# A two-layer diffusion backbone: the conditioning and first block of layer 0 traced in another order, with five pieces of the conditioning multiplied whole

## The chip, the cores and the metric

The kernel runs on one core of a Trainium2 chip, in one launch. The metric is device time in microseconds (us), as a median over runs. TensorE (PE) multiplies matrices, VectorE (DVE), ScalarE (ACT) and GpSimd (POOL) work element by element, SyncE (SP) issues nearly all transfers; each takes its instructions in order.

## The reference

The model has width 1024 and two layers over 256 context tokens and 2048 latent tokens. What matters here is how a layer starts: a conditioning vector goes through SiLU and a 1024 x 3072 matrix (`ada_w`), which gives shift, scale and gate; the input is normed, scaled and shifted to h; h goes into the layer's projections. All is float32.

```python
def ada_mod(cvec, w, b):
    m = jax.nn.silu(cvec) @ w + b
    shift, scale, gate = jnp.split(m, 3, axis=-1)
    return shift[:, None], scale[:, None], gate[:, None]

def modulate(x, mod, g):
    shift, scale, _ = mod
    return rmsnorm(x, g) * (1 + scale) + shift

def reference(...):
    for l in range(DEPTH):                       # 2 layers
        mp = ada_mod(c_ctx[None], ada_w[l], ada_b[l])
        ms = ada_mod(c, ada_w[l], ada_b[l])
        hp = modulate(xp, mp, norm_pre[l])       # 256 context tokens
        hs = modulate(xs, ms, norm_pre[l])       # 2048 latent tokens
        # l = 0: mla_pool_mixer (latent attention and pooling), l = 1: swa_mixer (banded attention)
        ...
        xp = xp + mp[2] * rmsnorm(op, norm_post[l])
        xs = xs + ms[2] * rmsnorm(os_, norm_post[l])
```

## The kernel before

Everything is kept transposed, features on the 128 partitions, so x is 8 chunks of 128 features. Tokens come in nine blocks of 256; block 0 is the context. Layer 0 makes two passes over the blocks: the first projects h to the low-rank queries, keys and values and to the pooling branch (chunks 0 to 4, the small matrix `wkr`, chunks 9 to 12 of `w0`), the second, with h made again, to the gates. Then comes attention, the output projection, and layer 1 in the same manner.

A float32 product is made from three float32r products: each operand is split into a high part, a rounded copy made on ScalarE, and a low part, the difference, made on VectorE or GpSimd (`split`, L55 to L57); `mm3` (L110) multiplies high by high, high by low and low by high. float32r matmuls are quick; a matmul on plain float32 operands needs no split.

The conditioning of layer 0 (L357 to L363) needs 16 pieces of `ada_w`, each 256 x 512 and 512 KB: four column groups j (2 and 3 hold the scale, 0 and 1 the shift, half of the features each), four quarters q of the 1024 rows. Each piece is loaded into one of 12 staging buffers (`wload`, L118), split, and multiplied with the SiLU of the two conditioning vectors by four matmuls (`ada_piece`, L137). After the fourth quarter of a group ScalarE copies the row out (`adarow`, L150), TensorE transposes it (L153), and VectorE adds the bias and, for the scale groups, forms (1 + scale) times the norm's weight (`amod`, L160). I number the pieces 0 to 15 in the order in which they are traced: groups 2, 0, 3, 1.

Block 0's h is made between them. `h_stats` (L168) loads x, squares it on ScalarE in two halves, adds the squares up on GpSimd, sums over the partitions with one fp32 matmul against ones (L186), forms r = 1/sqrt(mean square) in `rstd_of` (L90 to L100), stores r for the second pass (L188) and multiplies x by r (L190): on GpSimd for block 0, on VectorE for all later blocks. `h_mod` (L193) makes the high part as x m + s on ScalarE (L199), x m + s again on VectorE (L200), and the low part as their difference (L201). The buffer of x is single, so block 1's x is loaded when block 0's h is made. The buffer `sq` of the squares is single as well.

The text of the kernel doesn't fix the order of the instructions. A scheduler, which simulates a timeline of its own, sets for each engine and for SP's queue in what order they stand; instructions given to `keep_in_program_order` are not moved ahead. Semaphores carry the dependences. Before, the five loads of `w0` for chunks 0 to 4 and their splits (`w_in_load`, L366 to L370) are traced after all pieces, with low parts in turn on VectorE and GpSimd, and `h_mod` of block 0 after them.

## Time and profile before

| | |
|---|---|
| median of three runs | 3144.53 us (3138.21 to 3149.47) |
| the profiled execution | 3137.79 us, span 3135.7 us |
| mean granted TensorE clock | 0.984 of 2.4 GHz |
| busy share of the span | TensorE 96%, VectorE 70%, ScalarE 57%, GpSimd 50% |
| transfers | 375 MB, 120 GB/s on average, nearly all on SP's queue |

The span is the time from the first to the last instruction of the profiled execution; its own device time is 2 us longer. A busy share is an average over stages; the windows show it stage by stage. The timeline lists instructions by start, with the idle time before them and what ended it. A matmul's place in the pipe is best read from the distance between starts. An fp32 matmul shows as two records (x2).

### The profile page before, as it was taken

How to read it: one execution, taken by the hardware profiler on the slowest of the kernel's cores; microseconds unless marked ns; L12 is line 12 of the kernel's file. 1: busy time of each engine (PE TensorE's matmuls, PEld its weight loads, DVE VectorE, ACT ScalarE, POOL GpSimd, SP SyncE). 2: the span in 40 equal slices, each digit the busy share in tenths (PEclk: the TensorE clock that was granted, in tenths of full speed). 3: DMA queues.
4: the chain of work that ended last, by engine and by line, in shares of the span. 5: the costliest groups of instructions: out<-in, count | busy, mean ns of one | idle time of the engine just before them, and what ended most of it. 6: DMA issues, size and time to landing. Idle time of an engine off the chain costs nothing.

```text
span 3135.7 us, 53071 instructions
## 1 busy us (share of the span) xinstructions
PE 3001.8 (96%) x19120; PEld 2580.0 (82%) x19120; DVE 2183.6 (70%) x3976; ACT 1772.6 (57%) x3571; POOL 1579.3 (50%) x1406
## 2 busy tenths in 40 slices
PE   6999999999999999999999999999997999999998
PEld 4999988897777777777779999999996677666998
DVE  6656656986888888888856646677324888867555
ACT  6444444435877777777774433333324777775433
POOL 3223232215777787777875435555002555545554
PEclk8999999999999999999999999999998999999999
DMA  6544468743202202222215564436437354541554
GB/s 236 155 138 138 150 188 256 234 145 93 60 19 56 61 16 58 58 47 58 59 42 161 161 200 143 137 127 203 143 94 149 82 105 105 117 84 48 158 173 126
DMA packets 379681, 375.08 MB, mean 120 GB/s; under 512 B 27905, under 2 KB 344953, under 8 KB 378265
## 3 DMA queue, kind: packets, MB, share of 16 engines
q1 hardware_dynamic: 379404, 371.68, 41.8%
q8 instruction: 150, 2.46, 0.3%
q14 instruction: 115, 0.93, 0.1%
q10 hardware_dynamic: 12, 0.00, 0.0%
HBM read 242.13 MB, written 129.24 MB: 118 GB/s over the span
## 4 chain that ended last, share of the span: by engine, by line
PE 61%; DVE 12%; DMA 12%; ACT 5%; POOL 5%; issue 4%; SPq 1%; DVEq 0%; ACTq 0%; POOLq 0%
PE S L114 5%; PE S L115 5%; PE S L113 5%; PE S L598 4%; PE B L643 4%; PE A L640 4%; PE S L599 4%; PE S L600 4%; PE M L552 4%; PE M L114 3%; PE M L115 3%; PE M L113 3%; PE S L1172 2%; PE S L1171 2%; DVE xb L200 1%
## 5 line engine op out<-in xcount | busy, mean ns | idle before, releaser
L630 POOL TENSOR_TENSOR acc<-acc,ph 128x512 f32<-128x512 f32 x352 | 457.5, 1300 | 58.3 <-ACT ph L602 39.3
L602 ACT ACTIVATE ph<-S 128x512 fp32r<-128x512 f32 (+1 forms) x592 | 350.4, 592 | 177.9 <-PE S L600 170.0
L553 DVE TENSOR_REDUCE pm<-M 128x1 f32<-128x512 f32 (+1 forms) x656 | 390.9, 624 | 80.4 <-PE M L552 77.8
L614 DVE TENSOR_TENSOR pl<-S,ph 128x512 fp32r<-128x512 f32 (+1 forms) x496 | 334.3, 676 | 70.8 <-ACT S L607 63.2
L113 PE MATMUL S<-hh,wh 128*128 128x256 f32 x1296 | 370.2, 286 | 4.4 <-ACT wh L56 2.8
L114 PE MATMUL S<-hl,wh 128*128 128x256 f32 x1296 | 368.8, 285 | 4.1 <-DVE hl L201 4.1
L115 PE MATMUL S<-hh,wl 128*128 128x256 f32 x1296 | 368.7, 285 | 0.0
L607 ACT ACTIVATE S<-S 128x512 f32<-128x512 f32 (+1 forms) x496 | 292.0, 589 | 0.0
L113 PEld LDWEIGHTS S<-hh,wh 128*128 128x128 f32 x1296 | 249.3, 193 | 8.7 <-ACT wh L56 3.3
L114 PEld LDWEIGHTS S<-hl,wh 128*128 128x128 f32 x1296 | 249.8, 193 | 6.4 <-DVE hl L201 4.8
L115 PEld LDWEIGHTS S<-hh,wl 128*128 128x128 f32 x1296 | 249.5, 193 | 1.6 <-issue 0.3
L598 PE MATMUL S<-QS,KHL 97*128 97x512 f32 (+1 forms) x592 | 235.5, 398 | 2.0 <-DVE pl L614 1.3
L599 PE MATMUL S<-QS,KHL 96*128 96x512 f32 (+1 forms) x592 | 233.9, 395 | 0.0
L643 PE MATMUL B<-pl,VV 128*65 128x512 f32 (+1 forms) x592 | 228.7, 395 | 3.8 <-ACT ob L658 2.3
L600 PE MATMUL S<-QS,KHL 96*128 96x512 f32 (+1 forms) x592 | 232.3, 392 | 0.0
L552 PE MATMUL M<-KHL,QS 96*128 96x512 f32 (+1 forms) x656 | 221.2, 378 | 1.3 <-DVE pm L553 1.0
L640 PE MATMUL A<-ph,VV 128*128 128x512 f32 (+1 forms) x592 | 212.2, 397 | 2.5 <-ACT ph L602 2.0
L1189 POOL TENSOR_TENSOR bpl<-bpf,bph 128x512 fp32r<-128x512 f32 x136 | 178.0, 1309 | 58.0 <-ACT bpf L1177 50.4
L113 PE MATMUL M<-hh,oh 128*128 128x256 f32 x696 | 196.4, 283 | 3.3 <-ACT oh L56 3.3
L114 PE MATMUL M<-hl,oh 128*128 128x256 f32 x696 | 195.0, 280 | 0.0
L115 PE MATMUL M<-hh,ol 128*128 128x256 f32 x696 | 194.8, 280 | 0.0
L1181 POOL TENSOR_SCALAR_AFFINE_SELECT bpf<-bpf 128x512 f32<-128x512 f32 x120 | 79.5, 663 | 199.8 <-ACT bpf L1177 176.3
(380 smaller groups left out, 9496.9 us busy)
## 6 DMA issues: line engine op xcount, KB each, us to landing
q_d<-ehl SPq DMA_DIRECT2D x126, 256.0 KB
stg<-in_ada_w SPq DMA_DIRECT2D x48, 512.0 KB
xb<-in_xT SPq DMA_DIRECT2D x18, 1024.0 KB
xb<-x_d SPq DMA_DIRECT2D x18, 1024.0 KB
stg<-in_w SPq DMA_DIRECT2D x35, 512.0 KB
hh<-q_d SPq DMA_DIRECT2D x24, 512.0 KB
kn_d<-ehl SPq DMA_DIRECT2D x40, 256.0 KB
v_d<-ve SPq DMA_DIRECT2D x20, 512.0 KB
```

Of the source, the lines that this page charges most:

```text
L113: pe.matmul(ps, lhsT=wh, rhs=xh, start=i == 0, stop=False)
L114: pe.matmul(ps, lhsT=wh, rhs=xl, start=False, stop=False)
L115: pe.matmul(ps, lhsT=wl, rhs=xh, start=False, stop=i == n - 1)
L552: pe.matmul(ps[:, :w], lhsT=QS[u % 4][0:96, 0, 128 * s:128 * s + 128], rhs=KH[h % 2][0:96, c0:c0 + w], start=True, stop=True)
L553: dve.tensor_reduce(out=pms[u][:, s, i:i + 1], in_=ps[:, :w], axis=AX.X, op=ALU.max)
L598: pe.matmul(S[:, :n], lhsT=KH[s][0:97, kc], rhs=qh, start=True, stop=False)
L599: pe.matmul(S[:, :n], lhsT=KH[s][0:96, kc], rhs=ql[0:96], start=False, stop=False)
L600: pe.matmul(S[:, :n], lhsT=KL[s][0:96, kc], rhs=qh[0:96], start=False, stop=True)
L602: act.activation(out=ph[:, :n], in_=S[:, :n], func=AF.Exp, scale=MLA_SCALE)
L630: pool.tensor_tensor(out=acc[:, :n], in0=acc[:, :n] if ph0 is None else f(ph0)[:, :n], in1=f(ph)[:, :n], op=ALU.add)
L640: pe.matmul(A[:, :n], lhsT=V[:, kts[i], 0:128], rhs=ph[:, :n], start=i == 0, stop=i == nk - 1)
L643: pe.matmul(B[0:65, :n], lhsT=V[:, kts[i], 64:129], rhs=pl[:, :n], start=i == 0, stop=i == nk - 1)
```

## The change

All loads and steps of layer 0's conditioning and of block 0's h, and the first five loads of `w0`, now stand in one function, `first_block`, in a written order, and a new context `in_order` ties every instruction in it to the one before it on the same engine. The instructions of SP count too.

- Loads: `cs` first, then three pieces, then `ident`, `adab`, `vecs`, the fourth piece, x of block 0 and the other pieces. The store of r is traced before the five loads of `w0`. Loads for what follows are not issued before the last of `first_block` (`issue_after`).
- Five pieces (3, 7, 11, 14, 15) are not split: two fp32 matmuls each on the loaded data.
- The squares of block 0: GpSimd adds two pairs of chunks, four fp32 matmuls against ones add the rest, instead of one.
- h, for all blocks of both layers: VectorE forms (x m) r by chunk in one step (`h_scale`), ScalarE adds s for the high part, VectorE forms (x + s) minus the high part (`h_parts`). GpSimd no longer scales block 0.
- The low parts of `w0`'s first five chunks are all on VectorE.
- The sink loads of layer 1 and the two steps that use them, which stood in layer 0's start, are kept in program order.

```diff
+    @contextmanager
+    def in_order():
+
+        block = nc.cur_bb
+        last = block.bb.instructions[-1]
+        yield
+        traced = block.bb.instructions
+        i0 = next(k for k in reversed(range(len(traced))) if traced[k] is last) + 1
+        prev = {}
+        for ins in traced[i0:]:
+            if ins.engine in prev:
+                tc.add_manual_dep(ins, prev[ins.engine].name,
+                                  mybir.DependencyInfo(mybir.DependencyClass.NoSync, mybir.DependencyReason.DATA), reason="in_order")
+            prev[ins.engine] = ins
...
-    ident = const.tile([128, 128], F32, name="ident")
-    sp.dma_start(out=ident, in_=I["ident"])
     cs = const.tile([128, KD, 2], F32, name="cs")
     sp.dma_start(out=cs, in_=I["cs"])
+    ident = const.tile([128, 128], F32, name="ident")
     vecs = const.tile([128, 45], F32, name="vecs")
-    sp.dma_start(out=vecs, in_=I["vecs"])
     adab = const.tile([128, 2, 24], F32, name="adab")
-    sp.dma_start(out=adab, in_=I["adab"])
+
+    def const_load():
+        sp.dma_start(out=ident, in_=I["ident"])
+        sp.dma_start(out=adab, in_=I["adab"])
+        sp.dma_start(out=vecs, in_=I["vecs"])
...
-    def ada_piece(l, j, q, wh, wl, ep):
+    def ada_piece(l, j, q, wh, wl, ep, whole=None):
+
         if q == 0:
             adaps[l, j] = bank("M", 3)
         ps = adaps[l, j]
         for i in range(2):
             k = 2 * q + i
+            if whole is not None:
+                pe.matmul(ps[0:2], lhsT=scf[:, k], rhs=whole[:, i], start=False, stop=k == KD - 1)
...
-            (eng or dve).tensor_tensor(out=x[:, c], in0=x[:, c], in1=r.unsqueeze(1).to_broadcast([128, 4, 256]), op=ALU.mult)
...
-    def h_mod(hp, b, l, x):
+        return x, r
+
+    def h_tiles(hp):
+        return [hp.tile([128, KD, 256], F32R, tag=t, name=t, bufs=2) for t in ("hh", "hl")]
+
+    def h_scale(b, l, x, r, ks):
         j = 0 if b == 0 else 1
-        hi, lo = [hp.tile([128, KD, 256], F32R, tag=t, name=t, bufs=2) for t in ("hh", "hl")]
-        for c in (slice(0, 4), slice(4, 8)):
-            for k in range(c.start, c.stop):
-                m, s = amod[l][:, k, j:j + 1], mods[l][:, k, j:j + 1]
-                act.activation(out=hi[:, k], in_=x[:, k], func=AF.Identity, scale=m, bias=s)
-                dve.tensor_scalar(out=x[:, k], in0=x[:, k], scalar1=m, scalar2=s, op0=ALU.mult, op1=ALU.add)
-            dve.tensor_tensor(out=lo[:, c], in0=x[:, c], in1=f(hi)[:, c], op=ALU.subtract)
+        for k in ks:
+            dve.scalar_tensor_tensor(out=x[:, k], in0=x[:, k], scalar=amod[l][:, k, j:j + 1], in1=r, op0=ALU.mult, op1=ALU.mult)
+
+    def h_parts(b, l, x, hi, lo, ks):
+        j = 0 if b == 0 else 1
+        for k in ks:
+            sh = mods[l][:, k, j:j + 1]
+            act.activation(out=hi[:, k], in_=x[:, k], func=AF.Identity, bias=sh)
+            dve.scalar_tensor_tensor(out=lo[:, k], in0=x[:, k], scalar=sh, in1=f(hi)[:, k], op0=ALU.add, op1=ALU.subtract)
+
+    def h_mod(hp, b, l, x, r):
+        hi, lo = h_tiles(hp)
+        for ks in (range(0, 4), range(4, 8)):
+            h_scale(b, l, x, r, ks)
+            h_parts(b, l, x, hi, lo, ks)
...
-    h0 = {}
-    for i, (j, q) in enumerate([(j, q) for j in (2, 0, 3, 1) for q in range(4)]):
-        if i == 4:
-            h0[0] = h_stats(p0, 0, 0, xT, False, pool)
-        ada_piece(0, j, q, *wload(ad, *wslot(p0, i % 9), ada_src(0, j, q), bufs=12), ad)
-
 
     w_in = {}
 
-    def w_in_load(c, s, eng=None, stg=p0, bufs=2):
-        w_in[c] = wload(stg, *wslot(p0, s), W0[c], eng, bufs)
-
-    for c in range(5):
-        w_in_load(c, c, (dve, pool)[c % 2], ad, 12)
-    h0[0] = h_mod(p0, 0, 0, h0[0])
+    def w_in_load(c, s, eng=None, stg=p0, bufs=2, after=None):
+        w_in[c] = wload(stg, *wslot(p0, s), W0[c], eng, bufs, after=after)
+
+    def first_block():
+
+        todo = [(j, q) for j in (2, 0, 3, 1) for q in range(4)]
+        stgs, x0 = {}, []
+
+        def load(n):
+            if n == 3:
+                const_load()
+            if n < len(todo):
+                t = ad.tile([128, 1024], F32, tag="stg", name="stg", bufs=12).rearrange("p (k m) -> p k m", k=2)
+                sp.dma_start(out=t, in_=ada_src(0, *todo[n]))
+                stgs[n] = t
+            if n == 3:
+                x0.append(h_load(p0, 0, xT))
+
+        def piece(n, sub=True):
+            j, q = todo[n]
+            raw = stgs.pop(n)
+            if (j, q) in WHOLE:
+                ada_piece(0, j, q, None, None, ad, raw)
+                return
+            hi, lo = [t.rearrange("p (k m) -> p k m", k=2) for t in wslot(p0, 5 + n % 4)]
+            split(hi, lo, raw)
+            ada_piece(0, j, q, hi, lo, ad)
+
+        ahead = 9
+        for n in range(ahead):
+            load(n)
+        h, ss = None, bank("A", 1)[:, 0:256]
+        sqs = []
+
+        def square(i):
+            sq = p0.tile([128, 4, 256], F32, tag="sq", name="sq", bufs=1)
+            act.activation(out=sq, in_=x0[0][:, 4 * i:4 * i + 4], func=AF.Square)
+            pool.tensor_tensor(out=sq[:, 0:2], in0=sq[:, 0:2], in1=sq[:, 2:4], op=ALU.add)
+            sqs.append(sq)
+
+        def sums(i):
+            for k in range(2):
+                pe.matmul(ss, lhsT=ones, rhs=sqs[i][:, k], start=i == 0 and k == 0, stop=i == 1 and k == 1)
+
+        for n in range(len(todo)):
+            if n == 4:
+                square(0)
+            if n == 6:
+                square(1)
+            piece(n)
+            load(n + ahead)
+            if n == 5:
+                sums(0)
+            if n == 7:
+                sums(1)
+                r = rstd_of(p0, ss, [(0, 256, D)])
+                h_scale(0, 0, x0[0], r, range(0, 4))
+                h = h_tiles(p0)
+            if n in (9, 10):
+                h_parts(0, 0, x0[0], *h, range(2 * n - 18, 2 * n - 16))
+            if n == 12:
+                h_scale(0, 0, x0[0], r, range(4, 8))
+            if n == 13:
+                sp.dma_start(out=r_d[0][:, 0:256], in_=r)
+        w_in_load(0, 0, dve, ad, 12)
+        w_in_load(1, 1, dve, ad, 12)
+        h_parts(0, 0, x0[0], *h, range(4, 8))
+        for c in range(2, 5):
+            w_in_load(c, c, dve, ad, 12)
+        return h
+
+    WHOLE = [(2, 3), (0, 3), (3, 3), (1, 2), (1, 3)]
+    with in_order():
+        h0 = {0: first_block()}
+    first_loads = last_of(mybir.EngineType.SP)
...
-        sp.dma_start(out=sinkc, in_=I["sink"].rearrange("(h o) -> h o", o=1))
-        sp.dma_start(out=sinkb, in_=I["sink"].rearrange("(o h) -> o h", o=1).to_broadcast([128, 16]))
+        tc.keep_in_program_order(sp.dma_start(out=sinkc, in_=I["sink"].rearrange("(h o) -> h o", o=1)))
+        tc.keep_in_program_order(sp.dma_start(out=sinkb, in_=I["sink"].rearrange("(o h) -> o h", o=1).to_broadcast([128, 16])))
         for z in mx3:
-            dve.tensor_scalar(out=z[:, :, 2], in0=sinkb, scalar1=1.0 / SWA_SCALE, scalar2=None, op0=ALU.mult)
+            tc.keep_in_program_order(dve.tensor_scalar(out=z[:, :, 2], in0=sinkb, scalar1=1.0 / SWA_SCALE, scalar2=None, op0=ALU.mult))
```

SP's queue at the start, before (`stg` are staging buffers, `r_d` is the store of r, `in_w` are chunks of `w0`):

```order
L122 DMA stg<-in_ada_w 128x2x512 x4
L171 DMA xb<-in_xT 128x8x256
L122 DMA stg<-in_ada_w 128x2x512 x10
L379 DMA stg<-in_w0r 128x256
L122 DMA stg<-in_w 128x1024
L122 DMA stg<-in_ada_w 128x2x512
L1223 DMA sinkc<-in_sink 16x1
L1224 DMA sinkb<-in_sink 128x16
L122 DMA stg<-in_ada_w 128x2x512
L122 DMA stg<-in_w 128x1024 x5
L188 DMA r_d<-rs_y 128x256
```

and now:

```order
L416 DMA stg<-in_ada_w 128x2x512 x3
L85 DMA ident<-in_ident 128x128
L86 DMA adab<-in_adab 128x48
L87 DMA vecs<-in_vecs 128x45
L416 DMA stg<-in_ada_w 128x2x512
L200 DMA xb<-in_xT 128x8x256
L416 DMA stg<-in_ada_w 128x2x512 x12
L466 DMA r_d<-rs_y 128x256
L144 DMA stg<-in_w 128x1024 x5
L486 DMA stg<-in_w0r 128x256
L144 DMA stg<-in_w 128x1024
```

The store of r stood behind all loads of `w0`'s first chunks and now stands ahead of them; `w0r` and chunk 9 stand behind them.

ScalarE from the first piece on, with the semaphores each row waits for, before (`sq` is a half of the squares, `adarow` a finished row):

```order
L56 CAST wh<-stg 128x1024 [waits DMAHW5_49]
L56 CAST wh<-stg 128x1024 [waits DMAHW6_49]
L56 CAST wh<-stg 128x1024 [waits DMAHW7_49]
L179 ACTIVATE sq<-xb 128x1024 [waits DMAHW0_49]
L150 COPY adarow<-M 4x512 [waits PE_49]
L56 CAST wh<-stg 128x1024 [waits DMAHW1_49]
L56 CAST wh<-stg 128x1024 [waits DMAHW2_49]
L179 ACTIVATE sq<-xb 128x1024 [waits Activation_49,Pool_49]
L56 CAST wh<-stg 128x1024 [waits DMAHW3_49]
```

and now:

```order
L71 CAST wh<-stg 128x1024 [waits DMAHW2_49]
L71 CAST wh<-stg 128x1024 [waits DMAHW3_49]
L180 COPY adarow<-M 4x512 [waits PE_49]
L439 ACTIVATE sq<-xb 128x1024 [waits DMAHW0_49]
L71 CAST wh<-stg 128x1024 [waits DMAHW1_49,DVE_49]
L71 CAST wh<-stg 128x1024 [waits DMAHW2_49,DVE_49]
L439 ACTIVATE sq<-xb 128x1024 [waits PE_49,Pool_49]
L71 CAST wh<-stg 128x1024 [waits DMAHW3_49,DVE_49]
L180 COPY adarow<-M 4x512 [waits PE_49]
```

The first row copy stands ahead of the first square, and the second square waits for TensorE, which reads the first one.

VectorE from the norm to block 0's h, before (`wl` is a low part of a weight, `mod` and `amod` are shift and scale, `A` holds the sum of squares):

```order
L93 TENSOR_SCALAR A<-A 128x256
L57 TENSOR_TENSOR wl<-stg,wh 128x1024 x2
L98 SCALAR_TENSOR_TENSOR rs_t<-rs_y 128x256
L155 TENSOR_TENSOR mod_76<-M,adab 128x8
L99 TENSOR_TENSOR rs_t<-rs_t,A 128x256
L156 TENSOR_TENSOR mod_76<-M,mod_76 128x8
L57 TENSOR_TENSOR wl<-stg,wh 128x1024
L100 SCALAR_TENSOR_TENSOR rs_y<-rs_t,rs_y 128x256
L57 TENSOR_TENSOR wl<-stg,wh 128x1024 x2
L155 TENSOR_TENSOR mod_76<-M,adab 128x8
L156 TENSOR_TENSOR mod_76<-M,mod_76 128x8
```

and now:

```order
L111 TENSOR_SCALAR A<-A 128x256
L116 SCALAR_TENSOR_TENSOR rs_t<-rs_y 128x256
L117 TENSOR_TENSOR rs_t<-rs_t,A 128x256
L118 SCALAR_TENSOR_TENSOR rs_y<-rs_t,rs_y 128x256
L231 SCALAR_TENSOR_TENSOR xb<-xb,amod_75,rs_y 128x256 x4
L72 TENSOR_TENSOR wl<-stg,wh 128x1024 x2
L238 SCALAR_TENSOR_TENSOR hl<-xb,mod_73,hh 128x256 x2
L72 TENSOR_TENSOR wl<-stg,wh 128x1024
L238 SCALAR_TENSOR_TENSOR hl<-xb,mod_73,hh 128x256 x2
L185 TENSOR_TENSOR mod_73<-M,adab 128x8
L186 TENSOR_TENSOR mod_73<-M,mod_73 128x8
L190 SCALAR_TENSOR_TENSOR amod_75<-mod_73,vecs 128x4 x2
```

The norm is no longer interleaved with low parts: low parts 8, 9 and 10 stand behind r and the scaling.

On ScalarE the cast of chunk 9, which doesn't belong to `first_block`, now stands between the cast of piece 13 and the last row copy.

## Rows read from the trace of the kernel before

**Rows 1.** The page's first part, whole run: busy us (share) x instructions of each engine.
```profile
PE 3001.8 (96%) x19120; PEld 2580.0 (82%) x19120; DVE 2183.6 (70%) x3976; ACT 1772.6 (57%) x3571; POOL 1579.3 (50%) x1406
```

**Rows 2.** Windows of core 0, the kernel's start; its first row names the columns.
```profile
core 0: us, PE busy (x) PEld busy (x) DVE busy (x) ACT busy (x) POOL busy (x), PEclk, DMA share, GB/s
...
40.00:50.00 10.00, 7.28 (x34) 4.89 (x35) 9.61 (x6) 4.40 (x6) 4.89 (x2) 0.62 0.13 29
...
60.00:70.00 10.00, 10.00 (x81) 9.95 (x81) 3.76 (x3) 4.83 (x8) 3.72 (x3) 0.94 0.60 196
```

**Rows 3.** Timeline, SP's queue and ScalarE, loads: start us, us, what, [idle before <-releaser].
```profile
1.26 0.42 SPq L66 DMA_DIRECT2D cs<-in_cs  x1
...
2.67 1.97 SPq L122 DMA_DIRECT2D stg<-in_ada_w  x4
...
6.68 1.04 ACT L56 CAST wh<-stg 128x1024 fp32r<-128x1024 f32 x1 [1.87 <-DMA stg<-in_ada_w]
8.06 1.05 ACT L56 CAST wh<-stg 128x1024 fp32r<-128x1024 f32 x1 [0.34 <-DMA stg<-in_ada_w]
...
47.81 0.33 SPq L122 DMA_DIRECT2D stg<-in_w_uk  x1
...
51.63 1.04 ACT L56 CAST kh<-stg 128x1024 fp32r<-128x1024 f32 x1 [2.71 <-DMA stg<-in_w_uk]
```

**Rows 4.** Timeline, TensorE: start us, us, what.
```profile
13.88 0.39 PE L145 MATMUL M<-wh,sch 128*4 128x512 f32 x1
14.10 0.39 PE L144 MATMUL M<-wl,sch 128*2 128x512 f32 x1
...
23.84 1.22 PE L186 MATMUL A<-s,ones 128*128 128x256 f32 x2 [1.18 <-POOL s L185]
...
25.29 0.63 PE L145 MATMUL M<-wh,sch 128*4 128x512 f32 x1
25.71 0.63 PE L144 MATMUL M<-wl,sch 128*2 128x512 f32 x1
...
72.14 0.70 PE L186 MATMUL A<-s,ones 128*128 128x256 f32 x2 [0.88 <-POOL s L185]
...
72.79 0.28 PE L115 MATMUL S<-hh,wl 128*128 128x256 f32 x1
```

**Rows 5.** Timeline, VectorE, then ScalarE: single steps of the conditioning and of h.
```profile
30.06 0.42 DVE L100 SCALAR_TENSOR_TENSOR rs_y<-rs_t,rs_y 128x256 f32<-128x256 f32 x1
30.39 4.53 DVE L57 TENSOR_TENSOR wl<-stg,wh 128x1024 fp32r<-128x1024 f32 x2
...
55.26 1.22 DVE L201 TENSOR_TENSOR hl<-xb,hh 128x1024 fp32r<-128x1024 f32 x1
...
89.87 2.07 DVE L399 SCALAR_TENSOR_TENSOR cr<-cr,vecs,rs_y 128x256 f32<-128x256 f32 x5
...
26.86 0.57 ACT L150 COPY adarow<-M 4x512 f32<-4x512 f32 x1
...
33.88 2.08 ACT L199 ACTIVATE hh<-xb,mod,amod 128x256 fp32r<-128x256 f32 x4 [1.51 <-POOL xb L190]
```

**Rows 6.** Timeline, GpSimd: the scaling of block 0.
```profile
30.56 6.60 POOL L190 TENSOR_TENSOR xb<-xb,rs_y 128x1024 f32<-128x1024 f32 x2 [6.77 <-DVE rs_y L100]
```

**Rows 7.** Timeline, TensorE, SP's queue, ScalarE: from block 0's h to block 1's load.
```profile
68.29 0.28 PE L115 MATMUL S<-hh,wl 128*128 128x256 f32 x1
...
56.55 0.38 SPq L171 DMA_DIRECT2D xb<-in_xT  x1
...
63.82 1.06 ACT L179 ACTIVATE sq<-xb 128x1024 f32<-128x1024 f32 x1 [3.74 <-DMA xb<-in_xT]
```

**Rows 8.** Waits of TensorE: its line <- what ended it: total us, times, longest; whole run.
```profile
PE S L114 <- DVE hl L201: 4.1, 3, 2.7
```

**Rows 9.** Windows as in rows 2: layer 0's second pass, layer 1's second pass.
```profile
520.00:560.00 40.00, 37.55 (x278) 32.53 (x278) 36.85 (x66) 18.36 (x34) 11.39 (x8) 1.00 0.76 232
2240.00:2280.00 40.00, 40.00 (x345) 40.00 (x345) 13.21 (x20) 10.24 (x25) 0.00 (x0) 1.00 0.34 109
```

More of the change, by code (lines that the diff above doesn't have):

```diff
@@ L1 @@
-from contextlib import ExitStack
+from contextlib import ExitStack, contextmanager, nullcontext
 import numpy as np
@@ L115, in mm3, with last_of, wload @@
             pe.matmul(ps, lhsT=wl, rhs=xh, start=False, stop=i == n - 1)
-    def wload(stg, hi, lo, src, lo_eng=None, bufs=2, late=False):
+    def last_of(eng):
+        return next(i for i in reversed(nc.cur_bb.bb.instructions) if i.engine == eng)
+    def wload(stg, hi, lo, src, lo_eng=None, bufs=2, late=False, after=None):
         kk, m = src.shape[1], src.shape[2]
@@ L121, in wload @@
         raw = v(stg.tile([128, 1024], F32, tag="stg", name="stg", bufs=bufs))
-        d = sp.dma_start(out=raw, in_=src)
+        with tc.issue_after(after) if after is not None else nullcontext():
+            d = sp.dma_start(out=raw, in_=src)
         if late:
@@ L142, in ada_piece @@
             k = 2 * q + i
+            if whole is not None:
+                pe.matmul(ps[0:2], lhsT=scf[:, k], rhs=whole[:, i], start=False, stop=k == KD - 1)
+                continue
             if k:
@@ L148, in ada_piece, with ada_row @@
         if q == 3:
+            ada_row(l, j, ep)
+    def ada_row(l, j, ep):
+            ps = adaps[l, j]
             row = ep.tile([4, 512], F32, tag="adarow", name="adarow", bufs=1)
@@ L166, in hybrid_step, with h_load, h_stats @@
     r_d = [dram.tile([128, T], F32, name=f"r{l}_d") for l in range(2)]
-    def h_stats(hp, b, l, src, again, eng=None):
+    def h_load(hp, b, src):
+        x = hp.tile([128, KD, 256], F32, tag="xb", name="xb", bufs=1)
+        sp.dma_start(out=x, in_=src[:, :, 256 * b:256 * b + 256])
+        return x
+    def h_stats(hp, b, l, src, again):
         cols = slice(256 * b, 256 * b + 256)
-        x = hp.tile([128, KD, 256], F32, tag="xb", name="xb", bufs=1)
-        sp.dma_start(out=x, in_=src[:, :, cols])
+        x = h_load(hp, b, src)
         if again:
@@ L378, in wkr_load @@
         raw = p0.tile([128, 1024], F32, tag="stg", name="stg", bufs=2)[:, :256].rearrange("p (k m) -> p k m", k=KD)
-        sp.dma_start(out=raw, in_=I["w0r"])
+        with tc.issue_after(first_loads):
+            sp.dma_start(out=raw, in_=I["w0r"])
         split(wkr[:, :, 0:32], wkr[:, :, 32:64], raw)
@@ L385, in lw_load @@
         hi, lo = [lr.tile([128, 1024 if src.shape[1] == 2 else 768], F32R, name=f"{n}{t}") for t in "hl"]
-        lw[n] = wload(p0, hi, lo, src, eng)
+        lw[n] = wload(p0, hi, lo, src, eng, after=first_loads)
     norms = {}
@@ L488, in hybrid_step @@
             if b == 0:
-                w_in_load(9 + c, 5 + c)
+                w_in_load(9 + c, 5 + c, after=first_loads)
             spill(p0, block_mm("S", w_in[9 + c], h), vp_d[128 * c:128 * c + 128], cols)
```

4 lines of the change are left out of this document (1 added, 3 removed).

## The prediction

> **What bounds the kernel now.** I read the page's first part, then windows, then the timelines of the first 90 us engine by engine. TensorE is busy 96% of the span [rows 1], and from about 60 us on its windows are full [rows 2]: after that every microsecond by which the start ends earlier or later goes into the end. The start itself is not TensorE's. From 40 to 50 us VectorE is busy 9.61 of 10 us and TensorE 7.28 at a mean granted clock of 0.62 [rows 2], so TensorE waits there, and runs at its lower level (1.2 GHz) when it runs. Part of VectorE's work is slow: while GpSimd scales block 0 by r, 6.60 us for two operations [rows 6], two of VectorE's low parts take 4.53 us [rows 5], where one of this size takes 1.22 alone (the 128x1024 subtraction at 55.26) [rows 5]. So the question is when block 0's h is whole. Its last low part ends at 55.26 + 1.22 = 56.48 now [rows 5]; call this moment H. Two other marks: r, the reciprocal root that scales h, is done at 30.06 + 0.42 = 30.48 [rows 5], and the fifth chunk of the projection begins its last matmul at 68.29 [rows 7].
>
> **Prices.** A load of 512 KB follows the one before it by 8.06 - 6.68 = 1.38 us, and one that starts on an empty queue takes 51.63 - 47.81 = 3.82 us [rows 3]. A cast takes 1.04 [rows 3], a low part 1.22, a row's copy 0.57, a step of 128x256 on VectorE 0.42, or 2.07/5 = 0.41 in a series, a high part of h 2.08/4 = 0.52 [rows 5]; I add 0.1 per handover. An ordinary matmul of 512 columns takes 0.42 us at the lower level (25.29 to 25.71) and 0.22 at the upper one (13.88 to 14.10) [rows 4]. What a whole piece costs, two fp32 matmuls of 512 columns, is not in the trace. The nearest row is the fp32 sum over 256 columns: from 23.84 to 25.29 with one ordinary matmul of 0.42 in between, so 1.03 at the lower level; from 72.14 to 72.79 with one of 0.12, so 0.53 at the upper [rows 4]. For 512 columns the bounds are those figures (if all of it were fixed) and twice them; columns should dominate, so I take 0.9 (upper) and 1.8 (lower) for each, two per piece: 1.8 or 3.6 us, against four ordinary matmuls, 0.9 or 1.7.
> The Trainium skill, "TensorE: Matmul & The Clock Gate", section "Back-to-back issue gap", gives N/2.4 ns and a little more for N columns and sets no other price for fp32: by it a whole piece would cost about 0.45 us. The row of the sum, 0.53 for 256 columns, is some five times that rule, so the sum goes by the row.
>
> **From the start to r.** The first load moves from fifth to second place on SP's queue, so it is issued at 1.26 in place of 2.67 and its cast starts 1.41 earlier, at 5.27 [rows 3]. Piece 2 is there at 5.27 + 2 x 1.38 = 8.03; cast, low part and four matmuls at the lower level: 12.0. Piece 3, whole, at the upper level, which TensorE has at this time now [rows 4]: 13.8. Row copy 14.5. Only now comes ScalarE's square of x (the order holds it behind the copy), then casts 4 and 5: 17.5; low part 18.8; matmuls 19.8; the first two fp32 sums, 0.53 each: 20.9. **The second square waits for them**, since both squares use one buffer: 22.0. Behind it on ScalarE stands cast 6, though its load landed about 5 us before: 23.0; low part 24.3. TensorE has had nothing since 20.9, so I take the lower level: piece 6, 1.7, and whole piece 7, 3.6: 29.6. Row copy, four transposes: 30.8. Second pair of sums, 1.5 (between 1.1 and 2.1): 32.3. Six small steps to r at 0.42 with their handovers: **r at 35.4, 4.9 later than now**. With the upper level from piece 5 on it would be 32.6; with the lower one throughout, 39.
>
> **From r to H.** Scaling four chunks, 1.65; low parts 8 and 9, 2.4; two of h, 0.8; low part 10: 41.4. Piece 10: 42.7. Piece 11, whole: 44.5. Row copy 45.2. Cast 12, low part 12, four chunks scaled, low part 13: 50.3. Piece 13, 1.3; pieces 14 and 15, four fp32 matmuls between 0.9 and 1.8, taken 1.15: 56.2. Row copy 56.9; casts of chunks 0 and 1, four high parts of h, the last low part: **H at 61.4, 4.9 later than now**. The stretch is as long as before, 26.0 us against 26.0. What the change takes away (GpSimd's scaling, the slow low parts, five casts and low parts) is given back by whole pieces and by strict turns: each engine waits for the others in the traced order.
>
> **The loads behind r.** SP now stands before the store of r until r exists, and the five loads of w0 are behind it; before, they were issued first. At r = 35.4 the first lands at 39.7, the fifth at 45.2, the next one (chunk 9) at about 46.9. A cast of that chunk-9 load stands on ScalarE ahead of the last row copy. Both cost nothing: pieces 12 to 15, which end at 56.2, cover them. The cover is 9 us, and gone if r comes 9 us later still.
>
> **TensorE after H.** About 40 of the five chunks' 120 matmuls stand ahead of H in either order. The other 80 took 68.4 - 56.5 = 11.9 us. At 0.12 each they end at 71.0; with the first ones at the lower level, some 2 us later, 73.3. That is 2.6 to 4.9 later than now. Block 1's x is loaded when H frees its buffer: now issued at 56.55 and used at 63.82 [rows 7]; then issued at 61.5 on a queue with little on it, 3.82 + 1.38 = 5.2, used at 66.7, 2.9 later. I take **+3 us** for all that follows.
>
> **The rest.** h as (x m) r + s is also made for every later block, with 16 steps of 0.41 on VectorE and the same eight on ScalarE. TensorE waited for these low parts 4.1 us in the whole run, three times [rows 8], mostly in the start, so I cost it at nothing. The two sink loads and their two small operations move into layer 1, where VectorE may stand up to 3.8 us for a landing [rows 3]; it is busy 13.21 of 40 us there with TensorE full [rows 9], so nothing. The scheduler also shuffles neighbours in the projections of both layers, attention not at all; I allow 5 us either way. An execution like the profiled one (3137.79 us; span 3135.7) would take 3141. That execution lies 6.7 us under the median of the runs, 3144.53; so **3147.5** for the median. 0.3%, or 9.4 us, is about what a measurement of this kernel can tell from no change.
>
> **Rivals.**
> (a) *The lower level holds, and serial turns feed it.* With few matmuls per turn TensorE never rises between 14 and 60 us: r at 39, pieces 11, 13, 14 and 15 another 5 us: H at 70. Then the gain of shorter handling after it is lost as well: about +11, 3155.5. For it: TensorE was at the lower level at 23.84 [rows 4] and in much of 40 to 50 [rows 2] with more matmuls to do than it will have now. Against: whole pieces keep it occupied longer. It decides from r later than 38.
> (b) *Faster.* The upper level holds throughout: r at 32.6, H near 56, five chunks done at 65, -3; and the lighter h relieves layer 0's second pass, where VectorE is busy 36.85 of 40 us and TensorE idles 2.45 [rows 9]; four such windows make 9.8, of which 7 are had: -10, 3134.5. Against: TensorE's waits there don't name h [rows 8].
> (c) *Whole pieces cost one column a cycle*, and so five of them on the chain 0.45 to 0.9 instead of 1.8 to 3.6: some 7 us less, -4, 3140.5. This is where the section of the Trainium skill named under the prices leads. Against it the row of the fp32 sum.
> (d) *The order isn't held*: the scheduler may still put foreign steps between, as the chunk-9 cast shows. Then the start stays near its old length, 0 to +2; inside the forecast.
>
> **How the numbers follow.** Forecast with (d) 0.61, from 3139 to 3153; (a) 0.22; (b) 0.12; (c) 0.05. (c) and the forecast are within 0.3%, together 0.66; slower 0.22, faster 0.12. The range, 3133 to 3160, takes in (a) and just (b), with a tenth left out on either side for shuffled neighbours.
>
> **What would show it.** Right: r done at 34 to 37 us, the second square waiting for TensorE, first w0 cast after 39, H at 59 to 64, fifth chunk ending at 70 to 74, TensorE full after that. Wrong: a fp32 pair of 512 columns under 1.2 us, r before 32, w0 loads landing before r, H under 55; or a difference that arises after 100 us, which would be the scheduler's and not the start's.

## The result, and the profile after

The changed kernel takes 3171.27 us (3164.87 to 3173.92) against 3141.37 for the kernel before on the same chip: 1.0082 times as long, 95% interval 1.0064 to 1.0101, that is 20 to 32 us. The forecast was 3147.5, that is +3, with a range to 3160. The profiled execution took 3168.92 us, its span is 3167.2, 31.5 longer than before. All ratios here leave out one execution, of the kernel whose start is free (below): it took 8270.8 us at a mean granted clock of 0.599.

The start went as forecast up to H. The timelines of ScalarE, VectorE, TensorE and SP's queue in the changed kernel (start us, us, what, idle before):

```profile
21.72 1.06 ACT L439 ACTIVATE sq<-xb 128x1024 f32<-128x1024 f32 x1 [4.76 <-PE A L445]
...
67.92 1.06 ACT L213 ACTIVATE sq<-xb 128x1024 f32<-128x1024 f32 x1 [0.71 <-DMA xb<-in_xT]
...
35.04 0.42 DVE L118 SCALAR_TENSOR_TENSOR rs_y<-rs_t,rs_y 128x256 f32<-128x256 f32 x1
...
60.73 1.67 DVE L238 SCALAR_TENSOR_TENSOR hl<-xb,mod,hh 128x256 fp32r<-128x256 f32 x4
...
11.63 1.88 PE L167 MATMUL M<-stg,scf 128*2 128x512 f32 x4
...
27.05 3.58 PE L167 MATMUL M<-stg,scf 128*2 128x512 f32 x4
...
35.93 2.73 SPq L144 DMA_DIRECT2D stg<-in_w  x5
```

The second square waits 4.76 us for the first sums. r is done at 35.46 (before 30.48 [rows 5]), the loads of `w0` follow it, H is 60.73 + 1.67 = 62.40 (before 56.48), block 1's x is used at 67.92 (before 63.82 [rows 7]). A whole piece (two fp32 matmuls, four records) takes 1.88 us at the upper level and 3.58 at the lower.

Where the rest arises is read from the first and the last start of a line's matmuls. L598, now L705, is the score of layer 0's attention; L1172, now L1279, is one of layer 1's sliding-window attention. The view of one line, its TensorE instructions (count, duration in ns, first to last start), first the kernel before:

```profile
L598 PE MATMUL S<-QS,KHL x592: 278/396/632, 726.5 to 1623.3; 97*128 97x512 f32 x192, 97*128 97x256 f32 x6
...
L1172 PE MATMUL S<-hl,KBR x132: 389/396/795, 2375.7 to 2899.9; 96*128 96x512 f32 x132
```

The same in the changed kernel:

```profile
L705 PE MATMUL S<-QS,KHL x592: 278/397/632, 729.0 to 1626.1; 97*128 97x512 f32 x192, 97*128 97x256 f32 x6
...
L1279 PE MATMUL S<-hl,KBR x132: 389/397/795, 2385.3 to 2925.8; 96*128 96x512 f32 x132
```

At layer 0's attention the changed kernel is 2.5 us late, at its end 2.8: the forecast's 3. Then 6.8 are added up to the sliding-window stage, 16.3 in it (540.5 us against 524.2), 5.6 behind it; these and the 2.8 make the 31.5 (what of these is this one execution's own is told under what is left open). The stage is the largest part, and no line of its loop is in the diff.

In this stage 18 units of 128 queries go through three query buffers (`hh`, `mix0h` and `hh` again; a unit's buffer is loaded from `q_d` as soon as the scores of the unit three before have used it). Before a unit's scores, its *look-ahead* (L1115 and L1123 before, L1222 and L1230 now) multiplies its queries with its keys roughly, to find the row maxima; they go through a transfer (`bms`) into the low query buffer, and the scores wait for it. The scheduler chooses where between the scores of other units the look-ahead stands. Waits of TensorE (line <- what ended it: total us, times, longest), before:

```profile
PE S L1172 <- DMA hl<-bms: 8.6, 1, 8.6
PE M L1115 <- DMA hh<-q_d: 7.4, 3, 3.8
...
PE M L1115 <- DMA mix0h<-q_d: 2.4, 1, 2.4
```

The changed kernel:

```profile
PE M L1222 <- DMA hh<-q_d: 17.5, 8, 3.6
...
PE S L1279 <- DMA hl<-bms: 7.7, 1, 7.7
...
PE S L133 <- POOL wl L72: 3.1, 1, 3.1
...
PE M L1222 <- DMA o_d<-bo: 2.9, 1, 2.9
...
PE M L1222 <- DMA mix0h<-q_d: 2.3, 2, 1.6
```

The look-ahead now waits 17.5 + 2.9 + 2.3 = 22.7 us for its queries, against 9.8 (the 2.9, put down to `o_d`, stand like the others before the first look-ahead of a unit). Of TensorE as a whole, the windows that hold the stage (columns as in [rows 2]), before, then changed:

```profile
2375.00:2902.00 527.00, 487.06 (x2250) 345.28 (x2249) 403.34 (x910) 375.31 (x739) 262.87 (x262) 0.97 0.43 95
```

```profile
2385.00:2928.00 543.00, 490.67 (x2247) 348.18 (x2247) 397.85 (x910) 379.96 (x739) 262.04 (x262) 0.97 0.42 92
```

It idles 543.00 - 490.67 = 52.3 us in place of 527.00 - 487.06 = 39.9, and is busy 3.6 us longer with the same work. One unit shows how; the issue of its load on SP's queue and its first look-ahead on TensorE, before:

```profile
2533.20 0.60 SPq L1093 DMA_DIRECT2D hh<-q_d  x1
...
2558.38 0.60 PE L1115 MATMUL M<-KAR,hh 128*128 128x384 f32 x2
```

and in the changed kernel:

```profile
2541.36 0.59 SPq L1200 DMA_DIRECT2D hh<-q_d  x1
...
2549.31 0.59 PE L1222 MATMUL M<-KAR,hh 128*128 128x384 f32 x2 [2.68 <-DMA hh<-q_d]
```

Before, TensorE came to it 25.2 us after the issue; now 5.3 us after it, and stood 2.7 more until the queries were there, 7.95 in all. Counted in TensorE's order, from a buffer's last score to its next look-ahead, the units from the sixth on (the third reuse of a buffer and all later ones) have 16, 16, 16, 16, 16, 15, 12, 14, 10, 5, 2, 3, 3 score steps in between before, and 15, 10, 5, 2, 4, 5, 2, 5, 2, 3, 2, 4, 3 now. A score step is the scores of one unit with one key block, for four heads.

### The profile page after: what moved, and what is told of

Its sections match the earlier page's. It is cut to its first block, busy times and chain, and to the rows that moved or that the text cites. A ratio compares the mean times of both kernels' runs of the same rounds, so it can differ in the third digit from the quotient of the medians.

```text
span 3167.2 us, 53201 instructions
## 1 busy us (share of the span) xinstructions
PE 3017.5 (95%) x19126; PEld 2587.2 (82%) x19126; DVE 2112.9 (67%) x4119; ACT 1746.3 (55%) x3566; POOL 1549.2 (49%) x1399
## 4 chain that ended last, share of the span: by engine, by line
PE 53%; DVE 9%; DMA 9%; ACT 3%; issue 3%; POOL 3%; SPq 1%; DVEq 0%; POOLq 0%; ACTq 0%
PE S L705 4%; PE B L750 4%; PE A L747 4%; PE S L706 4%; PE S L707 4%; PE M L659 4%; PE S L132 4%; PE S L133 3%; PE S L131 3%; PE M L131 2%; PE M L132 2%; PE M L133 2%; DMA hh<-q_d 2%; DMA xb<-x_d 2%; PE S L1279 2%
## 5 line engine op out<-in xcount | busy, mean ns | idle before, releaser
L133 PE MATMUL S<-hh,wl 128*128 128x256 f32 x1296 | 368.0, 284 | 3.1 <-POOL wl L72 3.1
L133 PEld LDWEIGHTS S<-hh,wl 128*128 128x128 f32 x1296 | 249.0, 192 | 4.6 <-POOL wl L72 3.5
L705 PE MATMUL S<-QS,KHL 97*128 97x512 f32 (+1 forms) x592 | 235.8, 398 | 1.3 <-DVE pl L721 1.3
L133 PE MATMUL M<-hh,ol 128*128 128x256 f32 x696 | 195.8, 281 | 0.0
```

Of the source, the lines that this page charges most:

```text
L133: pe.matmul(ps, lhsT=wl, rhs=xh, start=False, stop=i == n - 1)
L705: pe.matmul(S[:, :n], lhsT=KH[s][0:97, kc], rhs=qh, start=True, stop=False)
```

## The experiments

Theory 1: the loss is the scheduler's new order in the sliding-window stage. Rivals: the start, by what it delays; the new formula of h itself; the sink loads.

**The look-ahead held where it is traced**, in the changed kernel and in the kernel before:

```diff
             q1_to(u + 1)
-            approx1(u, g, hp)
+            with tc.issue_after(last_of(mybir.EngineType.PE)) if now1[0] > 0 else nullcontext():
+                approx1(u, g, hp)
```

> The changed kernel, with the look-ahead of layer 1's sliding-window stage held no earlier than where it is traced: 20 score steps behind the last use of the query buffer that it waits for, where the changed kernel has 2 to 5 from the seventh unit on. Theory 1 (the loss after 1630 us is a new order of that stage, in which the look-ahead comes too close behind its query load; TensorE waits 17.5 us for those loads there, 7.4 before the change): the waits for query loads but the first go, the stage loses 13 to 17 us, 3154 to 3158 in all. Rival (the loads are late for another reason, such as a crowded queue, and the order only shows it): the waits move to other rows and the time stays within 4 us of 3171.

> The kernel before, with the same hold on the look-ahead and nothing else. Theory 1: the kernel before has the same waits in the last four units (1.8, 2.4, 1.8 us and a shorter one), so it gains 4 to 7 us: 3134 to 3137. Rival: it stays within 3 us of 3141, or loses by holding the look-ahead so late that the scores wait for its maximum.

Measured: 3223.66 us (1.0279, 1.0263 to 1.0295) and 3211.83 (1.0242, 1.0224 to 1.0259). Both far slower. TensorE's waits in the first of the two:

```profile
PE S L1280 <- DMA hl<-bms: 45.7, 10, 10.4
...
PE S L1280 <- DMA mix0l<-bms: 9.2, 4, 3.8
...
PE M L1222 <- DMA hh<-q_d: 4.4, 1, 4.4
```

The waits for queries went, all but the first one. But the place where it is traced, 20 score steps behind a buffer's last score, is too late for the maxima: the scores wait 54.9 us for them. The rival of the second expectation had allowed for that. The look-ahead has a window with two ends, and what I held it to lay outside. That the order of this stage is worth tens of us is shown; which side the changed kernel errs on is not yet.

**The new formula of h alone, and without it.** First the kernel before, with `h_scale` and `h_parts` for all blocks but the first; then the changed kernel, with the later blocks' `h_mod` as before. The edit of the second:

```diff
     def h_mod(hp, b, l, x, r):
+        j = 0 if b == 0 else 1
+        for c in (slice(0, 4), slice(4, 8)):
+            dve.tensor_tensor(out=x[:, c], in0=x[:, c], in1=r.unsqueeze(1).to_broadcast([128, 4, 256]), op=ALU.mult)
         hi, lo = h_tiles(hp)
-        for ks in (range(0, 4), range(4, 8)):
-            h_scale(b, l, x, r, ks)
-            h_parts(b, l, x, hi, lo, ks)
+        for c in (slice(0, 4), slice(4, 8)):
+            for k in range(c.start, c.stop):
+                m, s = amod[l][:, k, j:j + 1], mods[l][:, k, j:j + 1]
...
```

> The kernel before, with h made as (x m) r + s for every block but the first, and nothing of the new start or of the sink loads. Its sliding-window stage then stands in the same order as the changed kernel's (2 to 5 steps behind the query loads from the seventh unit on). Theory 1: that stage costs 16 us more, and the two places in layer 1's projection up to 6 more: 3155 to 3165, the most of the change's loss without its start. Rival (the new start causes the loss, by what it delays): 3138 to 3145.

> The changed kernel, with the later blocks' h made as before (x times r, then times m plus s; first block as changed). The sliding-window stage stands in a third order: 14, 10 and then 6 to 2 steps behind the query loads, between the other two. Theory 1: 3 to 6 us of the stage's loss come back and the start keeps its 2 to 3 us: 3158 to 3168. Rival (the formula itself costs the time, by its 16 smaller steps on VectorE for each block): 3141 to 3148, as all of the loss but the start's goes.

Measured: 3148.58 (1.0037, 1.0023 to 1.0050) and 3144.50 (1.0023, 1.0013 to 1.0033). Both lie below what theory 1 expected, the second where its rival had it. The line view of the kernel before with the new formula:

```profile
L622 PE MATMUL S<-QS,KHL x592: 278/396/628, 720.5 to 1617.0; 97*128 97x512 f32 x192, 97*128 97x256 f32 x6
...
L1196 PE MATMUL S<-hl,KBR x132: 389/396/792, 2369.2 to 2908.0; 96*128 96x512 f32 x132
```

Its stage takes 538.8 us, 14.6 more than before, with nothing of the new start in it: so the start is not the cause there. The total was too high in my expectation because the way to layer 0's attention gets 6.0 us shorter (720.5 against 726.5), which I had at nothing. The changed kernel with the old formula has a stage of 520.4 us, all of the loss back, though its look-ahead still waits 13.9 us: I had judged that third order by its step counts, and too hard. That the formula itself costs the time, as the rival says, doesn't go with a layer 0 that it shortens; the next two runs keep it and lose the loss. And the waits for queries are most of what an order does, not all of it: TensorE's idle time as a whole is back, 524.00 - 483.63 = 40.4 us in the window that holds the stage of the kernel with the old formula:

```profile
2385.00:2909.00 524.00, 483.63 (x2256) 343.89 (x2256) 400.17 (x912) 378.43 (x740) 261.75 (x262) 0.98 0.44 96
```

**The look-ahead held at 12 steps**, in the changed kernel, and in the kernel before with the new formula. `marks[k]` is the last TensorE instruction traced in step k; eight steps ahead of the traced place are 12 behind the buffer's last score:

```diff
-            approx1(u, g, hp)
+            with tc.issue_after(marks[now1[0] - 8]) if now1[0] >= 8 else nullcontext():
+                approx1(u, g, hp)
...
+        marks[k] = last_of(mybir.EngineType.PE)
```

> The changed kernel, with the look-ahead of the sliding-window stage held eight score steps before its traced place: 12 steps behind the last use of the query buffer from the sixth unit on (20 was too late for the maxima, 2 to 5 too early for the query loads). Theory 1 (a step lasts some 1.6 us, a query load 7.4 to 9 us from its issue to its use, the way from the last look-ahead to the score that needs its maximum about 10 us; 12 steps leave room on both sides): the ten late query loads, 18.6 us, go, no new wait for maxima comes, the stage falls from 542 to between 522 and 527 us, 3150 to 3156 in all. Rival (the stage is bound elsewhere, by VectorE's low parts): the waits for them grow as those for loads go, and it stays above 3162.

> The kernel before with the new formula of h in the later blocks (it reached the first attention score 6 us before the kernel before, and lost 14.5 in the sliding-window stage) and the hold at 12 steps. Theory 1: the 14.5 us come back and the 6 stay: 3130 to 3135, below both kernels. Rival (the 6 us of the first pass were given back by other places as well): 3137 to 3143.

Measured: 3147.97 (1.0031, 1.0021 to 1.0040) and 3133.05 (0.9981, 0.9968 to 0.9995). The changed kernel with this hold alone, the line view, then the waits:

```profile
L705 PE MATMUL S<-QS,KHL x592: 278/397/628, 726.8 to 1625.6; 97*128 97x512 f32 x192, 97*128 97x256 f32 x6
...
L1281 PE MATMUL S<-hl,KBR x132: 389/396/792, 2380.3 to 2901.6; 96*128 96x512 f32 x132
```

```profile
PE S L1281 <- DMA hl<-bms: 8.6, 1, 8.6
PE M L1223 <- DMA hh<-q_d: 4.6, 1, 4.6
```

The stage falls from 540.5 to 521.3 us, the look-ahead's waits from 22.7 to 4.6, and the scores wait for maxima once, as before the change. In the orders all units from the seventh on have 12 steps. Theory 1 holds (stage and time even lie a little under its 522 and 3150): of 0.82% lost, 0.51% go with this one edit (1.0082 to 1.0031, intervals apart). The second kernel is faster than the one before, as expected: 6 us from the formula, and a timely stage.

**The sink loads free to move**, in the changed kernel: `keep_in_program_order` taken from the four instructions.

> The changed kernel, with the two sink loads and the two operations behind them free to move again, as before. The order of everything else in the sliding-window stage stays that of the changed kernel. Theory 1 (VectorE stands 1.1 us for the sink load at 2250 us, where TensorE is full): within 4 us of 3171. Rival (the sinks' place pushes the loads behind them on SP's queue): 3150 to 3165.

Measured: 3166.81 (1.0092, 1.0071 to 1.0114; the changed kernel had 1.0082). By the ratios, whose intervals overlap, the sinks cost nothing that four runs can tell. In the changed kernel VectorE stands 1.1 us for the landing, where TensorE's window is full.

**The start without its edges**, the same program in the same traced order:

```diff
-    with in_order():
-        h0 = {0: first_block()}
+    h0 = {0: first_block()}
```

> The changed kernel, with its first block traced in the same order, but without the edges that hold every engine to it. TensorE's order differs from the changed kernel's in the first 600 instructions and in a few of layer 0's attention; the rest is the same. Theory 1 (the start's own cost is the 2 to 3 us that the first attention score is late, and turns are not dear): the first score moves by less than 3 us, 3168 to 3174. Rival (the hold costs the 12 us that the changed kernel is late at 130 to 175 us, and the rest of the first pass only happens to give some back): the first score comes 5 us sooner or more, 3160 to 3166.

Measured: 3139.10 (1.0003, 0.9989 to 1.0018), below even the rival's figure. Theory 1 falls here: the edges are dear. The timelines of ScalarE, VectorE and TensorE, then the line view:

```profile
17.04 1.06 ACT L439 ACTIVATE sq<-xb 128x1024 f32<-128x1024 f32 x1
...
24.33 0.42 DVE L118 SCALAR_TENSOR_TENSOR rs_y<-rs_t,rs_y 128x256 f32<-128x256 f32 x1
...
42.78 1.67 DVE L238 SCALAR_TENSOR_TENSOR hl<-xb,mod,hh 128x256 fp32r<-128x256 f32 x4
...
21.71 1.88 PE L167 MATMUL M<-stg,scf 128*2 128x512 f32 x4
```

```profile
L704 PE MATMUL S<-QS,KHL x592: 278/397/628, 711.3 to 1611.6; 97*128 97x512 f32 x192, 97*128 97x256 f32 x6
...
L1278 PE MATMUL S<-hl,KBR x132: 389/396/792, 2368.0 to 2911.8; 96*128 96x512 f32 x132
```

Nothing waits for the second square, r is done at 24.75, H is 44.45, 18 us sooner than with the edges and 12 sooner than before; the first attention score comes at 711.3, 17.7 sooner than with them. The stage is as long as in the changed kernel (543.8 us). TensorE's clock shows part of what the edges did, here 20 to 30 us, first with them, then without:

```profile
20.00:30.00 10.00, 6.37 (x14) 1.66 (x12) 1.46 (x1) 1.99 (x2) 1.27 (x1) 0.67 0.87 320
```

```profile
20.00:30.00 10.00, 8.69 (x32) 2.24 (x30) 9.44 (x18) 8.05 (x13) 0.00 (x0) 1.00 1.05 392
```

With the edges it is granted 0.67 to 0.86 in every 10 us from 10 to 60 us; without them 1.00 throughout these. So the change holds a gain of some 15 us in layer 0 (726.5 to 711.3), which the edges take back.

**Both edits together**, the start free and the look-ahead held at 12 steps.

> The two edits together: the changed start without the edges that hold every engine to it, and the look-ahead of the sliding-window stage held at 12 steps. The first brought the first attention score from 729.0 to 711.3 us, the second the stage from 542 to 523. Theory 1 (two losses in two places that know nothing of each other): they add, 3139 less 14 to 18, so 3120 to 3126, below both kernels. Rival (the 3139 of the free start is already past its loss in the stage, so the hold finds less there): 3130 or more.

Measured: 3125.37 us, 0.9948 times the kernel before (0.9934 to 0.9962). The two add, and the kernel beats both.

```profile
L704 PE MATMUL S<-QS,KHL x592: 278/396/792, 710.5 to 1606.8; 97*128 97x512 f32 x192, 97*128 97x256 f32 x6
...
L1280 PE MATMUL S<-hl,KBR x132: 389/395/792, 2357.4 to 2878.8; 96*128 96x512 f32 x132
```

First score at 710.5, stage 521.4 us: each what it was alone.

**Inside the held start**, three edits, each in the changed kernel with its edges. The first sums behind the first square; the store of r behind the loads of `w0`; and `WHOLE = []`, this with the hold at 12 steps:

```diff
             if n == 4:
                 square(0)
+                sums(0)
...
-            if n == 5:
-                sums(0)
```

> The changed kernel with its order held, but the first two fp32 sums traced right behind the first square, ahead of piece 4 in place of behind piece 5. Everything after the start stands as in the changed kernel. Theory 1 (the dearest turn is the second square, which waits 4.8 us on ScalarE for these sums and leaves TensorE idle and at its lower level): the second square starts near 17 in place of 21.7, r is done at 28 to 31 in place of 35.5, H at 55 to 58 in place of 62.4, and the end comes 4 to 7 us sooner, 3164 to 3167. Rival (other turns take it back, as ScalarE and VectorE wait for each other piece by piece): r comes sooner, but H stays over 60 and the time within 2 us of 3171.

> The changed kernel with its order held, but the store of r traced behind the five loads of the projection, so that they don't stand behind r on SP's queue. Theory 1 (the loads have a cover of 9 us, as their casts are held behind the last conditioning piece): the first of the five casts starts within 1 us of where it did, H stays at 61 to 63, 3168 to 3174. Rival (late loads of the projection hold up what comes behind them): H 58 or less, 3166 or less.

> The changed kernel with its order held and the look-ahead at 12 steps, with all 16 pieces of the conditioning split again and none whole; it stands against the run with that hold alone, 3148. Theory 1 (a whole piece on the chain costs 1.9 or 3.6 us on TensorE and saves a cast of 1.0 and a low part of 1.2 with their handovers, so it pays only where the clock is up): H between 60 and 66, the time within 5 us of 3148. Rival (whole pieces are the cost of the new start): H below 59 and 3143 or less.

Measured: 3154.70 (1.0050, 1.0030 to 1.0070), 3162.85 (1.0076, 1.0052 to 1.0100), 3134.99 (0.9984, 0.9971 to 0.9997). With the sums sooner (ScalarE, then VectorE):

```profile
18.09 1.06 ACT L439 ACTIVATE sq<-xb 128x1024 f32<-128x1024 f32 x1 [0.74 <-PE A L445]
...
28.95 0.42 DVE L118 SCALAR_TENSOR_TENSOR rs_y<-rs_t,rs_y 128x256 f32<-128x256 f32 x1
...
54.63 1.67 DVE L238 SCALAR_TENSOR_TENSOR hl<-xb,mod,hh 128x256 fp32r<-128x256 f32 x4
```

One traced place moved takes r from 35.46 to 29.37, H from 62.40 to 56.30 and the first score to 722.2, as theory 1 expected; the end gains somewhat more than the 4 to 7 us, 0.32% or 10 us by the two ratios, whose intervals meet at the edge. The store of r is worth nothing, as expected: the loads were issued from 20.18 on, in place of 35.93, and H stayed at 62.39. Its time, of two runs, lies under the 3168 of theory 1, but its ratio doesn't part from the changed kernel's. Without whole pieces H is 59.66, the first score 722.6; the time lies 13 us under the 3148 of the run with the hold alone, more than theory 1 allowed, though H is not below the rival's 59. By the profiled executions the two are 6.9 us apart: 4.2 at the first score and 4.5 in the stage, less some in between. Only the first is the start's: the stage stands in another order there (two units have 17 and 14 steps where the run with the hold alone has 12 and 12), so this pair doesn't compare whole pieces alone. Still H is 2.7 us under the lowest, and the first score 4.2 under the lowest, of all kernels with the changed kernel's start. In the held order, then, whole pieces cost a few us more than they save; what they do in the free order wasn't tried.

All runs in one table; times in us. The stage is the time from the first to the last start of L1172's row, the waits are those of the look-ahead's first line (L1115) for transfers.

| kernel | first attention score | stage | look-ahead's waits | ratio to before |
|---|---|---|---|---|
| before | 726.5 | 524.2 | 9.8 | 1 |
| changed | 729.0 | 540.5 | 22.7 | 1.0082 |
| changed, look-ahead at 20 steps | 730.8 | 605.6 | 4.4 | 1.0279 |
| before, look-ahead at 20 steps | 729.9 | 600.8 | 3.5 | 1.0242 |
| before, new formula | 720.5 | 538.8 | 22.0 | 1.0037 |
| changed, old formula | 731.9 | 520.4 | 13.9 | 1.0023 |
| changed, 12 steps | 726.8 | 521.3 | 4.6 | 1.0031 |
| before, new formula, 12 steps | 720.5 | 523.8 | 3.9 | 0.9981 |
| changed, sinks free | 732.5 | 537.6 | 21.7 | 1.0092 |
| changed, start free | 711.3 | 543.8 | 22.1 | 1.0003 |
| changed, start free, 12 steps | 710.5 | 521.4 | 3.6 | 0.9948 |
| changed, sums sooner | 722.2 | 540.2 | 21.1 | 1.0050 |
| changed, store of r later | 729.4 | 537.5 | 21.6 | 1.0076 |
| changed, none whole, 12 steps | 722.6 | 516.8 | 3.6 | 0.9984 |

The six kernels with the changed kernel's order of the stage take 537.5 to 543.8 us in it; those whose look-ahead is neither as early nor at 20 steps take 516.8 to 524.2. Kernels with the same order of TensorE up to the first score differ there: two with the order of before have 726.5 and 729.9, five with that of the changed kernel 726.8 to 732.5. So 3 us in one place of one execution say little, and the +2.5 of the changed kernel is within that; 720.5 (twice) and 711.3 and 710.5 are not.

## Why the prediction was wrong

The step that failed stands under "The rest": "The scheduler also shuffles neighbours in the projections of both layers, attention not at all; I allow 5 us either way." In layer 0's attention a few neighbours changed places, between some 1415 and 1435 us, and cost nothing (896.8 us from first to last score before, 897.1 now). In layer 1 the sliding-window stage was ordered anew, and this alone cost 16.3 us in the profiled execution, more than three times what I had allowed for all shuffling; the waits for queries are 13 longer (22.7 less 9.8). The hold at 12 steps, which leaves TensorE's order ahead of the stage as it was, takes it back (521.3 us). I had put one figure on all shuffling, without asking which stage stands close to a wait. That stage had shown it: the look-ahead waited 9.8 us for queries before the change already.

The other steps, in turn:

- *From the start to r, from r to H*: right, mark by mark. r at 35.46 for 35.4, the second square at 21.72 for about 21, H at 62.40 for 61.4, x of block 1 used at 67.92 for 66.7.
- *Whole pieces*: 1.88 us at the upper level and 3.58 at the lower, for the 1.8 and 3.6 taken from the row of the fp32 sum. The rule of the Trainium skill, "TensorE: Matmul & The Clock Gate", section "Back-to-back issue gap", by which a piece would take an estimated 0.45, is some four times too low for this piece; rival (c) falls with it.
- *The loads behind r cost nothing*: right, shown by the run with the store moved.
- *TensorE after H, +3 us for all that follows*: right at the first attention score (+2.5), but by luck. The forecast wanted TensorE full after H, and it was not (below), nor was it before the change, from 70 to 90 us. The sum of squares of the last block (L186, now L220) starts at 363.3 us where it had started at 357.2: 6.1 late, about what H was late (5.9), and not 3. From there to the first score the changed kernel takes 365.7 us against 369.3, and gives back 3.6.
- *h as (x m) r + s at nothing*: wrong with the start of before. The new formula alone reaches that sum at the same 357.2 and the first score 6.0 us sooner; 4.0 of them are one wait of TensorE for a low part on VectorE (`ve`, between 440 and 480 us) that falls from 4.4 to 0.4. Rival (b) had the size (7 us) and the engine; but the place is not the windows that it counted, as from 520 to 560 us TensorE is busy 37.24 us in place of 37.55, and the condition failed: with the held start the time still rose. The gain hangs on the order, too: the free start, with the same formula, takes 370.2 us from that sum (341.1) to the first score, no less than before.
- *The sinks at nothing*: right.
- *What the change takes away is given back by strict turns*: right, and larger than I saw. Rival (d) put a start that isn't held at 0 to +2; it is 15 us faster than before at the first score, and 16.1 at the sum named above. The turn I had marked, the second square that waits for the first sums, is a third of the 18 us (H from 62.40 to 56.30 when it goes).
- *Rival (a)* had the sign and nothing else: between 20 and 60 us TensorE was granted 0.67 to 0.84, so it did rise, and r came at 35.5, not past 38.
- *The last sentence of the prediction*, that a difference after 100 us would be the scheduler's, is what came.

TensorE after H, windows with the columns of [rows 2], before:

```profile
80.00:90.00 10.00, 9.16 (x74) 8.90 (x74) 9.90 (x18) 5.58 (x12) 0.00 (x0) 1.00 0.36 122
...
100.00:120.00 20.00, 20.00 (x155) 19.29 (x155) 14.22 (x31) 10.65 (x25) 6.26 (x7) 1.00 0.51 151
```

and in the changed kernel, where a gap of 2.4 us in the second row and 3.1 in the third, at a lower granted clock, stand behind H:

```profile
60.00:70.00 10.00, 10.00 (x85) 10.00 (x85) 7.45 (x10) 7.03 (x12) 0.94 (x1) 1.00 0.62 188
...
80.00:90.00 10.00, 7.60 (x53) 6.84 (x52) 9.54 (x19) 6.56 (x15) 1.31 (x2) 0.95 0.59 188
...
100.00:120.00 20.00, 16.94 (x114) 15.97 (x114) 9.57 (x21) 11.03 (x23) 7.33 (x7) 0.91 0.35 111
```

Left open: with the stage mended the changed kernel still stands at 1.0031, 11 us by medians, while its profiled execution, the fastest of its runs, is only 2.5 us longer than before's. Of the 6.8 us between layer 0's attention and the stage most are the execution's own: that stretch took 759.2 us, and 750.6 to 756.4 in the ten other kernels with the same order of TensorE there, against 752.4 before. It holds a new wait of 3.1 us for a low part on GpSimd (`S L133 <- POOL wl`), which some of those ten don't have; it was not taken away by an experiment of its own. The 5.6 us behind the stage are the execution's own too: TensorE's order there is that of before, and the other kernels with it take 233.9 to 238.3 us from the stage's last score to the end, against 235.8 before and 241.4. And why the scheduler orders that stage anew when the start or the formula of h changes was not followed; that each of the two does it is seen in the orders.

## What to carry to other kernels

Where a scheduler sets the order, the diff doesn't bound what moves: compare the order of every stage before and after, and for each that moved look at which transfers it waits for, and by how little they are on time now. Work that is done ahead of its use has a window, between the landing of what it needs and the deadline of what needs it; hold it inside by an edge to a step in its middle, and try more than one place (12 steps gained 19 us, 20 lost 65). And an edit that fixes the order of several engines at once makes each wait for the others' delays: here it took 18 us back from a change that was worth 15.

## What the runs showed of the hardware that I had not expected

A late transfer of 2.7 us in full TensorE work can cost more than 2.7 us. The changed kernel's windows around the look-ahead at 2549.31 (columns as in [rows 2]):

```profile
2540.00:2546.00 6.00, 6.00 (x28) 4.05 (x27) 4.91 (x10) 4.84 (x11) 2.25 (x3) 1.00 0.57 129
2546.00:2550.00 4.00, 1.32 (x7) 0.81 (x6) 0.24 (x1) 1.28 (x3) 1.86 (x2) 0.99 1.13 232
2550.00:2554.00 4.00, 4.00 (x14) 3.13 (x13) 2.58 (x7) 2.16 (x4) 0.50 (x1) 0.58 0.18 42
2554.00:2560.00 6.00, 6.00 (x31) 4.60 (x30) 5.67 (x19) 3.81 (x7) 3.29 (x4) 1.00 0.04 5
```

TensorE idles, and then runs at its lower level for some 4 us, granted 0.58: 14 matmuls in 4 us, where 31 go in the 6 behind. Not each wait does so. Of the eleven waits of the look-ahead for queries in this execution, five (3.6, 2.7, 2.3, 2.9 and 2.0 us long) stand before 4 us granted 0.57 to 0.65, and six (0.7 to 2.4 us) before 4 us at 1.00; in the last of the five, at 2782.57, the clock fell within the wait. A wait of 2.4 us, at 2585.31, is among the six and one of 2.3, at 2647.89, among the five, so length alone doesn't tell. The Trainium skill, "TensorE: Matmul & The Clock Gate", section "HAM oscillation — how this bites in real kernels", tells of a loop that falls to the lower level at every wait for a transfer; the trace agrees in kind, with five of these eleven waits.
